# In a head pair's attention preparation: the queries' rotation first, then key norms and value blocks in turn

## The chip, the core and the metric

The program runs on one core of a Trainium2 chip. The metric is the device time of one execution in microseconds (us). The kernel before takes 3843.91 us (median of three runs, 3839.26 to 3847.75).

## What is computed

The reference runs four residual blocks (a gated unit, an RWKV-7 scan, a latent attention, a second gated unit) and then a second network (a gated linear scan with a convolution, and a mixture of 16 experts) on 512 tokens of width 1024. The change touches the latent attention alone: 16 heads, 512 queries, 768 keys (256 of the context, 512 of the sequence), and both queries and keys are normalised over 192 features, 64 of which are rotated.

```python
def mla_project(h, w_in, q_norm, kv_norm, w_uq, w_ukv, qk_gain_q, qk_gain_k, need_q):
    ...
    q = (rms_norm(c_q, q_norm) @ w_uq).reshape(bsz, length, MLA_HEADS, MLA_QK_DIM)
    q = rms_norm(q, qk_gain_q)
    ...
    kv = (rms_norm(c_kv, kv_norm) @ w_ukv).reshape(bsz, length, MLA_HEADS, MLA_NOPE + MLA_VDIM)
    k_nope, v = jnp.split(kv, [MLA_NOPE], axis=-1)
    k = jnp.concatenate([k_nope, jnp.broadcast_to(k_rope[:, :, None, :], ...)], axis=-1)
    k = rms_norm(k, qk_gain_k)
...
    s = jnp.concatenate([jnp.einsum('bqhd,bkhd->bhqk', qp, k_ctx), jnp.einsum('bqhd,bkhd->bhqk', qr, k_rot)], axis=-1)
    p = jax.nn.softmax(s.astype(jnp.float32) * MLA_SCALE, axis=-1).astype(v.dtype)
    return jnp.einsum('bhqk,bkhd->bqhd', p[..., :n_ctx], v_ctx) + jnp.einsum('bhqk,bkhd->bqhd', p[..., n_ctx:], v)
```

## The kernel before

Float32 products are made of three passes over a high and a low part (`mm3`, L169): an operand is split by a ScalarE copy into the high part and a subtraction on VectorE (`split`, L165) or GpSimd (`gsplit`, L2164) into the low part.

The attention's stage (L2144 to L2594) walks over 64 units, a unit being one head and 128 queries. `scores(u)` (L2439) makes 128 x 768 scores in a PSUM tile `ps2`, of which there is one buffer, so the next unit's scores can't be written before this unit's exponential has read it. VectorE takes the row maximum (L2455) and scales it (L2456), ScalarE makes the exponential (L2458) and scales it by the reciprocal of its sum (L2461 on VectorE, L2462 on ScalarE). `trans(u)` (L2465) turns the probabilities with six TensorE transposes (L2475) in two parts, 512 and 256 wide, and splits them into `a_pt` (L166 on ScalarE, L167 on VectorE). `av` (L2487) multiplies two units by the values. Other PSUM tiles (`ps`) come from a ring of six banks.

`prep(i)` (L2209) prepares a pair of heads while the units of the pair before are worked on. It is a generator; each of its steps puts matmuls first and hands the engines that follow their work one step later (`Work.step`, `Work.after`). `fill` (L2554) takes steps of it between scores, products and transposes, paced by the cost that each `yield` states. No scheduler reorders anything: every engine runs its queue in the order in which the generators wrote it. The steps of a pair, in order:

- keys' and queries' projections (`k_part`, `q_part`), then `slow.append(k_rstd())` and the second head's queries;
- `k_rstd` (L2302): a chain of small VectorE instructions (L2304, L258 to L270; tiles `rk_x`, `rk_t`, `rk_y` of 128 x 12) that makes the keys' inverse norms, and two ScalarE copies (L2310) that spread them into tiles called `rx`. `trickle(1)` puts a piece of it behind every step, and `trickle(99)` (L2315) the rest at once;
- `rot()` (L2345): the queries' rotated part, one product with a permutation (L2348) and the sums `q_sum(2)`; then VectorE L2353 and L2367, ScalarE L2360, GpSimd L2352 and L2362;
- `keys(2)`, `keys(0)`, `keys(1)` (L2318): the keys' norms turned and broadcast by transposes (L2325, 512 and 256 wide), multiplied on VectorE (L2329 for the rotated part, L2332 for a head), split by ScalarE L2165 and GpSimd L2166 into `a_krr` or `a_kn`;
- `q_sum(1)`, sums of the queries' squares on TensorE (L2274);
- three value blocks (L2389): twelve matmuls each, split by ScalarE L2403 and VectorE L2405 into `a_v`. After the first, `slow.append(q_rstd())`: the chain of some 16 small VectorE instructions (L2377, L2379, L2382, L258 to L270, L2387; tiles `a_c`, `rq_x`, `rq_t`, `rq_y` of 128 x 8) that makes the queries' inverse norms `rqs`, one of which goes behind each step.

The first pair has no units to lie between. Where this text says pair 4, it is the fifth of eight, whose rotation stands at 2209.8 us.

Of the kernel before, what the change touches and what calls it, by code (L numbers as in the profile page):

```python
# [106 lines left out]
KD = 450  # L107
KTR = 0.5
RG = 0
ORD = "p201"  # L110
AHEAD = 0.6
AVP = 1
NTR = 1
# [5 lines left out]
class Net:  # L119
# [1834 lines left out]
    def mla(self):  # L1954
# [228 lines left out]
        slow = []  # L2183

        def trickle(n):

            while slow and n > 0:
                c = next(slow[0], None)
                if c is None:
                    slow.pop(0)  # L2190
                n -= 0 if n == 99 else c or 1
# [5 lines left out]
        def o_load(c):  # L2197
            t = t5()
            nc.sync.dma_start(t, d_o[c])
            s8 = mp.tile([P, 2, TX], F32R, name="cq", bufs=6) if c < 6 else mp.tile([P, 2, TT], F32R, name="ckv", bufs=2)[:, :, :TX]  # L2200
            S8.append((s8, t))
# [7 lines left out]
        def prep(i):  # L2209
# [59 lines left out]
            def q_sum(j):  # L2269
                sq = sqs.pop(j)  # L2270
                for t_ in range(4):
                    tk = slice(t_ * P, (t_ + 1) * P)
                    if j < 2:
                        nc.tensor.matmul(pq[:, 4 * t_ + j:4 * t_ + j + 1], sq[:, tk], self.ones[:, :1], start=True, stop=True)  # L2274
                    else:
                        nc.tensor.matmul(pq[:, 4 * t_ + 2:4 * t_ + 4], sq[:, tk], bones[:, 0:P:64], start=True, stop=True)
# [35 lines left out]

            slow.append(k_rstd())
            yield from q_part(1, q_head(1))
            trickle(99)  # L2315
            rk = R["rk"]

            def keys(j):  # L2318
                for s0, s1 in ((0, 4), (4, 6)):
                    rx_ = rx.pop(0) if j == 2 else None  # L2320
                    o, w = s0 * P, (s1 - s0) * P
# [46 lines left out]
                parts(1, r)  # L2368
                yield 0

            for c in ORD:
                yield from rot() if c == "p" else keys(int(c))
            q_sum(1)

            def q_rstd():
                c4 = tl("c4", (P, 4, 4), 2)
                V.tensor_copy(c4.rearrange("p t c -> p (t c)"), pq[:, :16])  # L2377
# [8 lines left out]
                R["rqs"] = tl("rqs", (P, 8), 2)  # L2386
                V.tensor_scalar(R["rqs"], rq, 192 ** -0.5, None, op0=OP.mult)  # L2387

            for t2 in range(3):  # L2389
                ps = self.psum()  # L2390
                for tt in range(2):
                    t_ = 2 * t2 + tt
# [11 lines left out]
                for j, vv in enumerate(R["v"]):  # L2404
                    V.tensor_tensor(vv[:, 1, ts, :], p4[:, :, j * P:(j + 1) * P], vv[:, 0, ts, :], op=OP.subtract)  # L2405
                if i == H // 2 - 1:
                    for c in ((0, 1, 2, 3), (), (4, 5, 6, 7))[t2]:
                        o_load(c)
                    for c in ((), (0, 1), (2, 3))[t2]:
                        o_split(c)  # L2410
                if t2 == 0:
                    slow.append(q_rstd())
                if t2 == 2:
                    for _ in range(2 if i < H // 2 - 1 else 1):
                        wnext()
                yield 0

        def out_first():

# [1519 lines left out]
```

## Time and profile before

| what | us |
|---|---|
| median of three runs | 3843.91 |
| the profiled execution | 3851.94 |
| its span | 3850.0 |
| preparation of the first pair's tail, then the 64 units | about 1958 to 2510 |
| TensorE busy in the whole span | 3335.9 (87%) |

The profiled execution lies 8.03 us over the median and 1.94 us over its own span. In the rows, a time is in us from the span's start; `PE` is TensorE, `DVE` VectorE, `ACT` ScalarE, `POOL` GpSimd. In the order of work, a bracket such as [1.57 <-ACT a_t L2310] says how long the engine stood idle before the instruction, and which instruction ended the idle time. An `x2` merges two instructions of a kind, and the duration is then that of both.

### The profile page before, as it was taken

The page shows a single profiled execution, that of the slowest core. Times are in us where ns is not written, and L with a number is a line of the kernel's source. Part 1 is how long each engine was busy: PE and PEld are TensorE (multiplying, and loading weights), DVE is VectorE, ACT ScalarE, POOL GpSimd, SP SyncE. Part 2 cuts the span into 40 slices and gives each one's busy share as a digit, 9 for nine tenths or more (in the row PEclk, how much of TensorE's full clock was granted, in tenths as well). Part 3 has the DMA queues.
Part 4 walks back from the last instruction along what each step waited for, and adds up shares of the span by engine and source line. Part 5 has one row for each costly group of instructions (what it writes and reads, how often), then busy time and mean ns, then how long its engine had stood idle before and what let it go on. Part 6 is the DMA issues. An engine that isn't in the chain of part 4 may idle for free. (4 is left out here: it accounts for less than half of the span.)

```text
span 3850.0 us, 63102 instructions
## 1 busy us (share of the span) xinstructions
PE 3335.9 (87%) x24502; PEld 2816.5 (73%) x24502; DVE 2505.5 (65%) x4375; ACT 1710.7 (44%) x2887; POOL 1317.8 (34%) x1559
## 2 busy tenths in 40 slices
PE   4999998888688889989989999899998886778883
PEld 3788887777577778767878878777886665667773
DVE  8777767453676666745445555556666789777777
ACT  4322213433455545645346666533232543346663
POOL 5131002220356666720033332301101556235555
PEclk8999998999797788989999999999999997779997
DMA  5444452246874343463422122345642210289883
GB/s 194 151 145 140 140 198 95 85 166 179 247 196 133 117 141 112 136 204 123 124 72 73 56 66 64 106 140 200 219 159 73 72 55 17 81 288 315 314 308 119
DMA packets 350861, 560.23 MB, mean 146 GB/s; under 512 B 170592, under 2 KB 226016, under 8 KB 350560
## 3 DMA queue, kind: packets, MB, share of 16 engines
q1 hardware_dynamic: 346960, 543.06, 43.5%
q0 software_dynamic: 3600, 13.11, 0.9%
q8 instruction: 194, 3.18, 0.3%
q14 instruction: 107, 0.88, 0.1%
HBM read 457.23 MB, written 88.36 MB: 142 GB/s over the span
## 5 line engine op out<-in xcount | busy, mean ns | idle before, releaser
L162 DVE TENSOR_TENSOR wlo<-wraw,whi 128x1024 fp32r<-128x1024 f32 x220 | 286.2, 1301 | 165.1 <-ACT whi L161 163.6
L171 PE MATMUL ps<-hl,whi 128*128 128x512 f32 (+1 forms) x992 | 363.7, 367 | 1.6 <-ACT hl L1946 1.6
L161 ACT CAST whi<-wraw 128x1024 fp32r<-128x1024 f32 x221 | 231.3, 1047 | 294.4 <-PE ps L172 183.1
L172 PE MATMUL ps<-hl,whi 128*128 128x512 f32 (+1 forms) x992 | 360.2, 363 | 2.0 <-DVE hl L1951 2.0
L173 PE MATMUL ps<-hl,wlo 128*128 128x512 f32 (+1 forms) x992 | 359.6, 363 | 2.6 <-DVE wlo L162 2.6
L3583 ACT CAST e_wsp<-mraw 128x1024 fp32r<-128x1024 f32 x204 | 212.3, 1050 | 105.1 <-issue 52.5
L3584 DVE TENSOR_TENSOR e_wsp<-mraw,e_wsp 128x1024 fp32r<-128x1024 f32 x136 | 187.3, 1399 | 73.0 <-ACT e_wsp L3583 71.6
L3584 POOL TENSOR_TENSOR e_wsp<-mraw,e_wsp 128x1024 fp32r<-128x1024 f32 x68 | 180.0, 2656 | 129.6 <-ACT e_wsp L3583 59.2
L173 PEld LDWEIGHTS ps<-hl,wlo 128*128 128x128 f32 x992 | 187.3, 189 | 34.9 <-DVE wlo L162 3.4
L172 PEld LDWEIGHTS ps<-hl,whi 128*128 128x128 f32 x992 | 187.3, 189 | 34.1 <-DVE hl L1951 4.1
L171 PEld LDWEIGHTS ps<-hl,whi 128*128 128x128 f32 x992 | 187.3, 189 | 31.8 <-ACT hl L1946 1.9
L1522 POOL TENSOR_TENSOR s_tmp<-s_N,s_P 128x15 f32<-128x15 f32 (+4 forms) x360 | 126.6, 352 | 167.8 <-DVE s_N L1506 141.5
L207 DVE SCALAR_TENSOR_TENSOR araw<-araw,conds 128x1024 f32<-128x1024 f32 x128 | 157.8, 1238 | 24.7 <-DMA araw<-ada 24.0
L171 PE MATMUL ps<-whi,hl 128*128 128x512 f32 x320 | 131.8, 412 | 27.5 <-ACT hl L404 25.8
L617 POOL TENSOR_SCALAR v<-v,vr_y 128x256 f32<-128x256 f32 x70 | 93.9, 1359 | 155.8 <-DVE vr_y L270 155.8
L171 PE MATMUL ps<-s,whi 128*128 128x512 f32 (+1 forms) x384 | 138.6, 361 | 0.0
L172 PE MATMUL ps<-s,whi 128*128 128x512 f32 (+1 forms) x384 | 136.7, 356 | 0.0
L173 PE MATMUL ps<-s,wlo 128*128 128x512 f32 (+1 forms) x384 | 136.6, 356 | 0.2 <-DVE wlo L162 0.2
L167 DVE TENSOR_TENSOR a_pt<-ps,a_pt 128x512 fp32r<-128x512 f32 (+1 forms) x128 | 69.2, 554 | 102.3 <-ACT a_pt L166 102.3
L172 PE MATMUL ps<-wlo,hl 128*128 128x512 f32 x320 | 131.8, 412 | 4.5 <-DVE wlo L162 4.3
L173 PE MATMUL ps<-whi,hl 128*128 128x512 f32 x320 | 131.6, 411 | 1.4 <-DVE hl L411 1.3
L1523 POOL TENSOR_TENSOR s_P<-s_P,s_tmp 128x15 f32<-128x15 f32 (+4 forms) x360 | 121.4, 337 | 28.2
(932 smaller groups left out, 10195.2 us busy)
## 6 DMA issues: line engine op xcount, KB each, us to landing
mraw<-moe_w SPq DMA_DIRECT2D x204, 512.0 KB, 5.3
araw<-ada SPq DMA_DIRECT2D x144, 512.0 KB, 3.9
wraw<-sgu_v SPq DMA_DIRECT2D x40, 512.0 KB, 3.4
wraw<-rw_in SPq DMA_DIRECT2D x40, 512.0 KB, 4.8
d_n<-ff SPq DMA_DIRECT2D x48, 384.0 KB, 5.2
s_fn<-d_n SPq DMA_DIRECT2D x24, 768.0 KB, 6.5
wraw<-sgu_out SPq DMA_DIRECT2D x34, 512.0 KB, 4.2
wraw<-sgu_u SPq DMA_DIRECT2D x32, 512.0 KB, 4.6
```

The costliest lines, as they stand in the source:

```text
L161: self.nc.scalar.copy(hi[:, :cols], t[:, :cols])
L162: (eng or self.nc.vector).tensor_tensor(lo[:, :cols], t[:, :cols], hi[:, :cols], op=OP.subtract)
L167: (eng or self.nc.vector).tensor_tensor(lo, src, hi, op=OP.subtract)
L171: mm(out, lh, rh, start=start, stop=False)
L172: mm(out, lh, rl, start=False, stop=False)
L173: mm(out, ll, rh, start=False, stop=stop)
L207: self.nc.vector.scalar_tensor_tensor(junk, w, 0.5, c, op0=OP.mult, op1=OP.mult, accum_out=out)
L617: e.tensor_scalar(vt[g][:, t, :], vt[g][:, t, :], r[:, t:t + 1], None, op0=OP.mult)
L1522: TTG(o, N[:, None, ts, s].to_broadcast([P, nj, nt]), Pm[:, js, s:s + 1].to_broadcast([P, nj, nt]), op=OP.mult)
L1523: TTG(Pm[:, js, ts], Pm[:, js, ts], o, op=OP.subtract)
L3583: S.copy(hl[:, 0, :], raw)
L3584: (G if j % 3 == 2 else V).tensor_tensor(hl[:, 1, :], raw, hl[:, 0, :], op=OP.subtract)
```

## The change

In every pair: `rot()` comes directly behind the second head's queries, then `q_sum(1)`, then the rest of `k_rstd` (`trickle(99)`), then `q_rstd` is handed out, and then `keys(2)`, the first value block, `keys(0)`, the second value block, `keys(1)`, the third. Before, `trickle(99)` stood ahead of `rot()`, the three `keys` followed one another, and the value blocks stood behind all of them. In the last pair the loads of finished heads (`o_load`) are spread over the three value blocks as 2, 2 and 4 instead of 4, 0 and 4. No instruction's kind, size or engine is changed.

```diff
             slow.append(k_rstd())
             yield from q_part(1, q_head(1))
-            trickle(99)
-            rk = R["rk"]
 
             def keys(j):
+                rk = R["rk"]
...
-            for c in ORD:
-                yield from rot() if c == "p" else keys(int(c))
-            q_sum(1)
-
             def q_rstd():
...
-            for t2 in range(3):
+            def values(t2):
                 ps = self.psum()
...
                 if i == H // 2 - 1:
-                    for c in ((0, 1, 2, 3), (), (4, 5, 6, 7))[t2]:
-                        o_load(c)
                     for c in ((), (0, 1), (2, 3))[t2]:
                         o_split(c)
-                if t2 == 0:
-                    slow.append(q_rstd())
+                    for c in ((0, 1), (2, 3), (4, 5, 6, 7))[t2]:
+                        o_load(c)
...
+            yield from rot()
+            q_sum(1)
+            trickle(99)
+            slow.append(q_rstd())
+            for j, t2 in ((2, 0), (0, 1), (1, 2)):
+                yield from keys(j)
+                yield from values(t2)
```

(`ORD` was "p201": the rotation, then keys 2, 0, 1.) Line numbers in the changed kernel are one lower up to L2315; behind that they differ by more: L2309 is the copy into `rx`, L2459 the exponential, L2463 its scaling, L2397 and L2399 the split of a value block, L2327 and L2330 the keys' multiplications.

ScalarE in pair 4, from the copies into `rx` on. Before:

```order
L2310 COPY a_t_22289<-rk_y 128x512
L2310 COPY a_t_22291<-rk_y 128x256
L2458 ACTIVATE a_p,a_sm<-ps_22272,a_mx,a_rqs 128x768
L2462 ACTIVATE a_p<-a_p,a_sm 128x768
L2360 CAST a_qrr<-a_t_22160 64x512 x2
```

Now:

```order
L2459 ACTIVATE a_p,a_sm<-ps_22272,a_mx,a_rqs 128x768
L2309 COPY a_t_22303<-rk_y 128x512
L2309 COPY a_t_22305<-rk_y 128x256
L2463 ACTIVATE a_p<-a_p,a_sm 128x768
L2358 CAST a_qrr<-a_t_22160 64x512 x2
```

The two copies moved from ahead of a unit's exponential to behind it.

ScalarE in pair 4 between the next two exponentials. Before:

```order
L2458 ACTIVATE a_p,a_sm<-ps_22351,a_mx,a_rqs 128x768
L2462 ACTIVATE a_p<-a_p,a_sm 128x768
L2165 CAST a_krr<-a_t_22377 64x256 x2
L2165 CAST a_kn<-a_knf 128x512
L2165 CAST a_kn<-a_knf 128x256
L166 CAST a_pt<-ps 128x4x128
L2165 CAST a_kn<-a_knf 128x512
L166 CAST a_pt<-ps 128x2x128
L2458 ACTIVATE a_p,a_sm<-ps_22441,a_mx,a_rqs 128x768
```

Now:

```order
L2459 ACTIVATE a_p,a_sm<-ps_22358,a_mx,a_rqs 128x768
L2463 ACTIVATE a_p<-a_p,a_sm 128x768
L2164 CAST a_krr<-a_t_22390 64x256 x2
L2397 CAST a_v<-ps 128x256 x2
L2164 CAST a_kn<-a_knf 128x512
L165 CAST a_pt<-ps 128x4x128
L2164 CAST a_kn<-a_knf 128x256
L165 CAST a_pt<-ps 128x2x128
L2459 ACTIVATE a_p,a_sm<-ps_22471,a_mx,a_rqs 128x768
```

A value block's two casts stand ahead of the keys' casts, and the keys' 256-wide cast stands between the two casts of the probabilities.

VectorE in the same place, from the reciprocal to the next maximum. Before:

```order
L2461 RECIPROCAL a_sm<-a_sm 128x1
L2329 TENSOR_TENSOR a_t_22377<-krot,ps 128x256
L2332 TENSOR_TENSOR a_knf<-a_knf,ps 128x512
L2332 TENSOR_TENSOR a_knf<-a_knf,ps 128x256
L2495 SCALAR_TENSOR_TENSOR a_o<-ps,a_z 128x256
L167 TENSOR_TENSOR a_pt<-ps,a_pt 128x4x128
L2332 TENSOR_TENSOR a_knf<-a_knf,ps 128x512
L167 TENSOR_TENSOR a_pt<-ps,a_pt 128x2x128
L2455 TENSOR_REDUCE a_mx<-ps_22441 128x1
```

Now (twelve of its rows; two more small ones and `a_pt` 128x2x128 follow before the maximum):

```order
L2327 TENSOR_TENSOR a_t_22390<-krot,ps 128x256
L259 TENSOR_SCALAR rq_t<-rq_x 128x8
L2399 TENSOR_TENSOR a_v<-ps,a_v 128x256 x2
L261 TENSOR_SCALAR rq_y<-rq_t 128x8
L262 TENSOR_SCALAR rq_x<-rq_x 128x8
L2330 TENSOR_TENSOR a_knf<-a_knf,ps 128x512
L265 TENSOR_TENSOR rq_t<-rq_y 128x8
L2496 SCALAR_TENSOR_TENSOR a_o<-ps,a_z 128x256
L267 TENSOR_TENSOR rq_t<-rq_t,rq_x 128x8
L166 TENSOR_TENSOR a_pt<-ps,a_pt 128x4x128
L269 SCALAR_TENSOR_TENSOR rq_y<-rq_t,rq_y 128x8
L2330 TENSOR_TENSOR a_knf<-a_knf,ps 128x256
```

The value block's subtractions came ahead of the keys' multiplication, the keys' second multiplication behind the first half of `a_pt`, and the queries' chain between them.

## Rows read from the trace of the kernel before

**Rows 1.** Busy time by engine, 2000 to 2450: busy (x count), TensorE's clock, DMA.

```profile
core 0: us, PE busy (x) PEld busy (x) DVE busy (x) ACT busy (x) POOL busy (x), PEclk, DMA share, GB/s
2000.00:2450.00 450.00, 408.76 (x2562) 357.78 (x2561) 244.74 (x616) 280.69 (x551) 161.37 (x139) 0.96 0.24 68
```

**Rows 2.** TensorE's waits, 1958 to 2460: waiting line, releaser, total us, times, longest.

```profile
PE ps L2325 <- ACT a_t L2310: 19.5, 8, 5.7
PE ps L2325 <- DVE a_t L2329: 6.8, 6, 1.5
PE ps L171 <- DVE a_pt L167: 6.7, 3, 2.3
PE ps L171 <- ACT a_p L2458: 6.5, 11, 2.3
PE ps L2325 <- DVE a_pt L167: 4.4, 4, 1.5
PE ps L2220 <- ACT a_t L2232: 1.7, 1, 1.7
```

**Rows 3.** TensorE in order of time, pair 4: start, us, instruction, idle before.

```profile
2213.71 1.11 PE L2325 MATMUL ps<-ident,a_t 128*128 128x128 f32 x4 [1.57 <-ACT a_t L2310]
...
2233.65 0.50 PE L171 MATMUL ps<-a_kn,a_qn 128*128 128x512 f32 x1 [0.43 <-ACT a_p L2458]
...
2241.68 0.48 PE L171 MATMUL ps<-a_kn,a_qn 128*128 128x512 f32 x1
```

**Rows 4.** ScalarE in order of time, pair 4, four exponentials and what lies between.

```profile
2213.04 0.92 ACT L2310 COPY a_t<-rk_y 128x512 f32<-128x512 f32 x2 [4.11 <-DVE rk_y L270]
2214.22 0.99 ACT L2458 ACTIVATE a_p<-ps,a_mx,a_rqs 128x768 f32<-128x768 f32 x1 [0.26 <-DVE a_mx L2456]
...
2215.54 0.94 ACT L2462 ACTIVATE a_p<-a_p,a_sm 128x768 f32<-128x768 f32 x1 [0.23 <-DVE a_sm L2461]
...
2224.20 0.99 ACT L2458 ACTIVATE a_p<-ps,a_mx,a_rqs 128x768 f32<-128x768 f32 x1 [1.67 <-DVE a_mx L2456]
...
2226.35 0.82 ACT L2165 CAST a_krr<-a_t 64x256 fp32r<-64x256 f32 x2
...
2228.03 0.58 ACT L166 CAST a_pt<-ps 128x512 fp32r<-128x512 f32 x1
2229.96 0.62 ACT L2165 CAST a_kn<-a_knf 128x512 fp32r<-128x512 f32 x1 [1.35 <-DVE a_knf L2332]
2230.48 0.37 ACT L166 CAST a_pt<-ps 128x256 fp32r<-128x256 f32 x1
2232.52 0.99 ACT L2458 ACTIVATE a_p<-ps,a_mx,a_rqs 128x768 f32<-128x768 f32 x1 [1.67 <-DVE a_mx L2456]
...
2234.97 0.64 ACT L2403 CAST a_v<-ps 128x256 fp32r<-128x256 f32 x2
...
2239.50 0.99 ACT L2458 ACTIVATE a_p<-ps,a_mx,a_rqs 128x768 f32<-128x768 f32 x1 [2.58 <-DVE rq_t L260]
```

**Rows 5.** VectorE in order of time, pair 4.

```profile
2228.64 0.69 DVE L167 TENSOR_TENSOR a_pt<-ps,a_pt 128x512 fp32r<-128x512 f32 x1 [1.58 <-ACT a_pt L166]
2229.25 0.68 DVE L2332 TENSOR_TENSOR a_knf<-a_knf,ps 128x512 f32<-128x512 f32 x1
2230.88 0.42 DVE L167 TENSOR_TENSOR a_pt<-ps,a_pt 128x256 fp32r<-128x256 f32 x1 [0.96 <-ACT a_pt L166]
2231.22 0.95 DVE L2455 TENSOR_REDUCE a_mx<-ps 128x1 f32<-128x768 f32 x1
...
2235.64 0.76 DVE L2405 TENSOR_TENSOR a_v<-ps,a_v 128x256 fp32r<-128x256 f32 x2 [1.53 <-ACT a_v L2403]
```

**Rows 6.** First pair, in order of time: TensorE, then VectorE, then GpSimd.

```profile
1965.75 1.54 PE L2325 MATMUL ps<-ident,a_t 128*128 128x128 f32 x6 [5.65 <-ACT a_t L2310]
...
1978.64 0.94 DVE L2382 COPY a_c<-a_c 128x8 f32<-128x8 f32 x1
...
1982.26 0.17 DVE L266 TENSOR_TENSOR rq_t<-rq_y 128x8 f32<-128x8 f32 x1
...
1976.30 3.96 POOL L2166 TENSOR_TENSOR a_kn<-a_knf,a_kn 128x512 fp32r<-128x512 f32 x4
```

More of the change, by code (lines that the diff above doesn't have):

```diff
@@ L109 @@
 RG = 0
-ORD = "p201"
 AHEAD = 0.6
```

## The prediction

> **What bounds the kernel now.** I read the busy times of the attention's stage first, then the list of what TensorE waited for, then the order of work of each engine around one rotation. From 2000 to 2450 us TensorE is busy 408.76 of 450 us at a mean clock of 0.96 [rows 1]; the stage ends when TensorE's queue ends, so only its idle time (41 us) and its slow stretches can change. The waits are few and all lie around the rotation and the keys: 19.5 us for the copies of the key norms (L2310, once per pair, 5.65 us of it in the first pair [rows 6]), 6.8 and 4.4 us in the keys' transposes, which wait for PSUM banks that VectorE reads late, 6.7 us of products that wait for the split probabilities, and 6.5 us of scores that wait for an exponential [rows 2].
>
> The last of these is the row to look at. The scores' PSUM tile has one buffer, so each unit's scores wait for the exponential of the unit before. Call the four exponentials of pair 4 E0 (2214.22, beside the rotation), E1 (2224.20), E2 (2232.52) and E3 (2239.50) [rows 4]. The scores behind E2 start at 2233.65 after 0.43 us of waiting for it [rows 3]: in the middle of the preparation the chain of ScalarE and VectorE from one exponential to the next is already as long as TensorE's own work. E1 to E2 is 8.32 us. The next scores, at 2241.68, carry no wait [rows 3]: E3 came 2.18 us before them, and that stretch of 8.03 us is TensorE's.
>
> **The change part by part.** No instruction is added or removed, so what counts is the place of each in its queue. Pairs 1 to 7 lie among units, the first does not.
>
> (a) The copies into the key-norm tiles now stand behind E0 on ScalarE. They take 0.92 us and were hidden ahead of E0; there ScalarE now waits 0.23 us less for the reciprocal [rows 4], so everything behind E0 comes 0.92 - 0.23 = 0.69 us later. On VectorE two small instructions of the queries' chain now stand ahead of E1's maximum, at 0.17 us each [rows 6]: 0.34 us. E0 itself comes some 0.2 us earlier, since the last small instruction of the keys' chain moves behind its maximum (0.17 us by the same row). Sum: 0.8 us later at E1. TensorE's wait for these copies becomes longer too (they came 1.18 us before E0, now 1 us behind it), but that costs nothing of its own: the queue is then bound by E1 and E2 anyway.
>
> (b) E1 to E2 is the main term. What must happen there in a row, because each engine takes its queue in order, is this. From E1 to the cast of the rotated keys: 2224.20 to 2226.35, 2.15. That cast: 0.82. The value block's casts until VectorE can subtract: 2234.97 to 2235.64, 0.67. The subtractions: 0.76. The keys' multiplication until its cast: 2229.25 to 2229.96, 0.71. That cast until the cast of the probabilities: 2229.96 to 2230.48, 0.52. From there to VectorE: 2228.03 to 2228.64, 0.61. To the keys' second multiplication: 2228.64 to 2229.25, 0.61. Its cast, and the next cast of probabilities, 256 wide: no more than the 0.71 and 0.52 of the 512-wide ones; I take 0.5 and 0.3. To VectorE: 2230.48 to 2230.88, 0.40. To the maximum: 0.34. To E2: 2231.22 to 2232.52, 1.30 [rows 4, 5]. Together 9.7, and four small instructions of the queries' chain between them, some 0.5 at 0.1 to 0.17 each: 10.2 us, against 8.32. Before, the value block was not in this stretch, and one keys' multiplication of the two was ready ahead of time. Cost 1.9 us, and since the scores behind E2 wait for E2 already, all of it comes through.
>
> (c) E2 to E3 has the same row without the rotated keys' cast: 9.7 - 0.8 + 0.4 = 9.3 us. Before it was 6.98 us and hidden under TensorE's 8.03. The scores behind E3 therefore come about 1.2 us later once more. TensorE has the same work behind it in both kernels, and runs without a wait there, so it doesn't win the time back.
>
> (d) What the value blocks fill. Moved between the keys, one block covers the products' wait and the keys' waits for banks. This saves TensorE's idle time at those rows, but the scores that follow wait for E2 and E3, so it is worth nothing while (b) and (c) hold. If they didn't, it would be the first rival.
>
> (e) The queries' chain meets GpSimd. L2382, a copy of 128 x 8, took 0.94 us while GpSimd worked through four subtractions (3.96 us), and an instruction of the same size took 0.17 us at 1982.26, when those were over [rows 6]. Before, most of this chain ran behind the keys' subtractions; now it runs among them and on the way to E1, E2 and E3. An instruction that meets one pays up to 0.94 - 0.17 = 0.8 us. Four or five stand on the way; most find GpSimd idle, since its subtraction follows a cast that VectorE waits beside. Bounds 0 and 4 us per pair; I take 0.5, near the lower one, since at most one of them falls inside a subtraction in the row of (b).
> The Trainium skill, page "SBUF — State Buffer", section "Who interferes with whom", says that an instruction of VectorE with two SBUF inputs, or a copy or scalar operation in a two-port mode, and one of GpSimd that reads SBUF exclude each other for the whole instruction. The 0.94 us row agrees with it, and by that rule every small instruction of the chain is open to such a wait, which speaks against moving the chain here.
>
> Per pair: 0.8 + 1.9 + 1.2 + 0.5 = 4.4 us, between 2.5 (a part of (a) and (c) absorbed by small overlaps) and 6.5 (two or three stalls of (e), and scores at a slower clock behind the longer waits). Seven pairs: 31 us, from 17 to 46.
>
> (f) The first pair. TensorE waited 5.65 us there for the key norms [rows 6]. The rest of the keys' chain now stands behind the rotation's addition, which waits for GpSimd, and then meets four of GpSimd's subtractions of the rotated queries: between 1.3 us (addition and multiplication alone) and 5 us later. Against it, TensorE fills some 1.6 us of the wait with the queries' sums, and the queries' norms are ready earlier, which saves up to the 1.7 us for which L2220 waited behind the first exponential [rows 2], and a stretch at slow clock behind it, about as much again. From -4 to +4; I take +0.5.
>
> (g) The last pair's loads go to the same queue in twos instead of fours, earlier than they are used. Taken as zero: no row of the waits shows TensorE held by them [rows 2].
>
> Sum: 31 + 0.5, about 31 us. On the profiled execution's 3851.94 that is 3883; that execution lies 8.03 us over the median, so against the median of 3843.91 it is 3875. Own range: 17 - 4 to 46 + 4, 3857 to 3894.
>
> **The rivals.**
>
> *The blocks fill the holes, and the exponentials keep up.* If the row of (b) is shorter than I added up, because casts and subtractions overlap more than one engine's order lets me see, TensorE stays the bound, and the waits for banks and probabilities go: 6.8 + 6.7 + 4.4, with the 1.7 of the first pair some 20 us. That gives 3824. It decides itself at E1 to E2: at or under 8.3 us it holds. For it: TensorE is the busiest engine by far (408.76 against 280.69 for ScalarE [rows 1]). Against it: every step of (b) hangs on the one before or stands behind it in its queue.
>
> *It evens out.* (b) holds but (c) doesn't, the units behind regain part, and the filled holes and the first pair's gain return the rest: 7 x 1.9 less about 10 us, 3845 to 3848.
>
> *The stalls of (e) are the rule.* Each small instruction on the way meets a subtraction: four times 0.8 per pair more than taken, less the 0.5: 2.7 x 7 = 19 us on top, 3894, and with slower clock behind the longer holes up to 3905.
> The Trainium skill's page "SBUF — State Buffer", same section, would make this the expected case wherever the two engines' work overlaps.
>
> **How the numbers follow.** Forecast 0.67, first rival 0.13, second 0.12, third 0.08. One can tell about 0.2%, 7.7 us, from no change for this kernel. Faster is the first rival, 0.13. The second is within 0.2% but for a sixth of it, which is slower: same 0.10. Slower is the rest: 0.77. The range runs from no change, with half of what can be told below it, to the third rival's lower end: 3840 to 3894, leaving out the first rival and most of the third, some 0.2. The time is the forecast's, 3875.
>
> **What would show it.** In pair 4 of the changed kernel: E1 to E2 near 10 us (8.3 now), E2 to E3 near 9.3 (7.0 now), and scores behind E2 and E3 that wait 2 to 4 and about 1 us for an exponential; TensorE's waits for L2310 up, for L2329 and the probabilities down, those for the exponential from 6.5 to over 25 us. The copies into the norm tiles start right behind E0. The prediction is wrong if E1 to E2 stays near 8.3 us, or if the stage from the first rotation to the last product gets shorter.

## The result, and the profile after

The changed kernel takes 3880.16 us, the median of five runs (3868.86 to 3887.28), against 3843.91 us (3839.26 to 3847.75): the ratio is 1.0095, with a 95% interval of 1.008 to 1.0109. That is 36 us more, between 31 and 42. The profiled execution of the changed kernel has a span of 3880.5 us.

Runs of one kernel differ by ten microseconds and more in the parts of the program that nothing here touches: in the profiled executions of this study the first rotation starts anywhere from 1938 to 1964 us. So beside each time stands a second measure that excludes those parts, the stretch from the first exponential of the attention stage to its last one (64 of them). It is 517.48 us before and 548.01 us after: 30.5 us of the 36 are there. Another 2.2 us lie in the first pair, between its rotation and the first exponential (27.15 us before, 29.37 us after, from starts of L2348 and L2458 before, L2346 and L2459 after). Lines have moved by one to eight numbers: L2458 is now L2459, L2310 is L2309, L2329 is L2327, L2403 is L2397, L2405 is L2399.

First the busy time of a stretch as long as in [rows 1]. The columns are those of that group.

```profile
1999.00:2449.00 450.00, 396.34 (x2419) 350.78 (x2419) 230.00 (x579) 262.45 (x513) 145.69 (x127) 0.92 0.21 59
```

TensorE is busy 396.34 us where it was busy 408.76, its mean clock is 0.92 in place of 0.96, and it finishes 2419 matmul records in place of 2562. TensorE's waits from 1958 to 2500 us, against [rows 2]:

```profile
PE ps L2323 <- ACT a_t L2309: 31.3, 8, 10.0
PE ps L170 <- ACT a_p L2459: 23.0, 8, 3.1
PE ps L2476 <- DVE a_t L2327: 8.8, 6, 2.0
PE ps L170 <- DVE a_v L2399: 4.3, 7, 0.7
PE ps L170 <- ACT cq L165: 3.2, 1, 3.2
```

The waits for the key norms' copies grew from 19.5 to 31.3 us, those of scores for an exponential from 6.5 to 23.0. The waits of [rows 2] for banks and for split probabilities (6.8, 6.7 and 4.4) are no longer in the list, but others took their place: the transposes of the probabilities wait 8.8 us for a bank that the rotary keys' multiplication (L2327) still reads, and matmuls wait 4.3 us for one that a value block's subtraction (L2399) still reads. Pair 4 on TensorE, against [rows 3]:

```profile
2229.88 1.11 PE L2323 MATMUL ps<-ident,a_t 128*128 128x128 f32 x4 [2.69 <-ACT a_t L2309]
...
2250.72 0.80 PE L170 MATMUL ps<-a_kn,a_qn 128*128 128x512 f32 x1 [3.12 <-ACT a_p L2459]
...
2260.19 0.48 PE L170 MATMUL ps<-a_kn,a_qn 128*128 128x512 f32 x1
```

The scores behind E2, which had 0.43 us to wait, wait 3.12 us. ScalarE in the same pair, against [rows 4]:

```profile
2228.24 0.99 ACT L2459 ACTIVATE a_p<-ps,a_mx,a_rqs 128x768 f32<-128x768 f32 x1 [5.07 <-DVE rk_y L269]
...
2229.23 0.91 ACT L2309 COPY a_t<-rk_y 128x512 f32<-128x512 f32 x2
2230.04 0.94 ACT L2463 ACTIVATE a_p<-a_p,a_sm 128x768 f32<-128x768 f32 x1
...
2239.51 0.99 ACT L2459 ACTIVATE a_p<-ps,a_mx,a_rqs 128x768 f32<-128x768 f32 x1 [2.40 <-DVE a_mx L2457]
...
2249.59 0.99 ACT L2459 ACTIVATE a_p<-ps,a_mx,a_rqs 128x768 f32<-128x768 f32 x1 [1.76 <-DVE rq_y L269]
...
2258.58 0.99 ACT L2459 ACTIVATE a_p<-ps,a_mx,a_rqs 128x768 f32<-128x768 f32 x1 [1.67 <-DVE a_mx L2457]
```

E0, E1, E2 and E3 are 11.27, 10.08 and 8.99 us apart, where they were 9.98, 8.32 and 6.98. The copies stand right behind E0. E4 to E7 are the exponentials of the four units behind E3, up to the next pair's E0.

All kernels of this study side by side, in starts of the exponentials of pair 4 (the last interval of the turn before it, then its first three, then the sum from E1 to E7). The same intervals repeat in pairs 5 and 6 within a few hundredths in most kernels; pairs 2 and 3 had a first interval of only 8.84 us in the kernel before. The column from E1 to E7 is pair 4's alone and differs between the pairs, as said below. The e, g and h kernels and k1 are edits of the changed kernel and keep its spread of the last pair's loads, also where they are described as the kernel before with one change.

| kernel | first to last | E7 to E0 | E0 to E1 | E1 to E2 | E2 to E3 | E1 to E7 | ratio of times, 95% |
|---|---|---|---|---|---|---|---|
| before | 517.5 | 10.93 | 9.98 | 8.32 | 6.98 | 45.3 | 1 |
| after | 548.0 | 10.75 | 11.27 | 10.08 | 8.99 | 48.5 | 1.0095 (1.0080 to 1.0109) |
| e1_norms_first | 545.6 | 10.94 | 10.76 | 10.06 | 8.99 | 48.5 | 1.0086 (1.0058 to 1.0113) |
| e2_chain_late | 542.0 | 10.73 | 10.44 | 9.71 | 9.12 | 48.6 | 1.0070 (1.0043 to 1.0097) |
| e3_keys_in_a_row | 540.7 | 10.72 | 11.22 | 9.49 | 6.90 | 48.7 | 1.0054 (1.0033 to 1.0074) |
| e4_turns_alone | 541.1 | 10.94 | 9.97 | 9.59 | 9.12 | 48.5 | 1.0094 (1.0066 to 1.0121) |
| g1_one_turn | 532.8 | 10.93 | 9.98 | 9.59 | 6.48 | 46.9 | 1.0035 (1.0018 to 1.0051) |
| g2_late_split | 540.7 | 10.73 | 11.23 | 9.33 | 7.86 | 48.4 | 1.0074 (1.0052 to 1.0096) |
| h1_copies_late | 519.6 | 10.74 | 10.45 | 8.31 | 6.91 | 45.5 | 1.0015 (0.9995 to 1.0034) |
| f2_chain_quick | 516.4 | 11.71 | 9.97 | 8.32 | 6.98 | 45.3 | 1.0015 (0.9997 to 1.0032) |
| f3_plain_keys_first | 520.6 | 10.93 | 9.21 | 9.08 | 6.98 | 46.1 | 1.0007 (0.9989 to 1.0025) |
| k1_after_filled | 547.7 | 10.73 | 11.25 | 10.07 | 9.00 | 48.5 | 1.0098 (1.0072 to 1.0123) |
| k2_before_filled | 516.5 | 10.93 | 9.98 | 8.32 | 6.98 | 45.3 | 0.9989 (0.9972 to 1.0005) |
| m1_chain_before_weights | 497.3 | 8.09 | 9.96 | 8.32 | 6.98 | 45.3 | 0.9912 (0.9892 to 0.9932) |

Each ratio is against runs of the kernel before in the same job, whose medians lay between 3837.75 and 3853.20 us. An expectation that names a time is therefore judged by its distance from the kernel before.

### The profile page after: what moved, and what is told of

It reads as the page before. It is cut to its first block, busy times and chain, and to the rows that moved or that the text cites. A ratio compares the mean times of both kernels' runs of the same rounds, so it can differ in the third digit from the quotient of the medians.

```text
span 3880.5 us, 63131 instructions
## 1 busy us (share of the span) xinstructions
PE 3345.7 (86%) x24502; PEld 2825.3 (73%) x24502; DVE 2510.3 (65%) x4375; ACT 1711.8 (44%) x2887; POOL 1320.8 (34%) x1559
```

## Experiments: which part of the change costs

The theory: the turns of keys and values cost most, the late copies and the early chain of the query norms a little each. The rival: one of the moved chains is the cause, and the turns are harmless.

**e1_norms_first.** The changed kernel with the key norms ahead of the rotation again:

```diff
-            yield from rot()
-            q_sum(1)
             trickle(99)
+            yield from rot()
+            q_sum(1)
```

> The changed kernel with one thing put back: the rest of the key-norm chain and its two ScalarE copies are issued ahead of the rotation again; the turns of keys and values, and the early query norms, stay. Theory (each moved piece pays in the interval of its own, and the turns pay most): in pairs 2 to 7 the first interval between exponentials falls from 11.26 us to 10.2 to 10.5, the second and third stay at 10.1 and 9.0, the first wait of TensorE for the copies in the first pair falls from 9.96 to about 5.7; seven times 0.8 to 1.0 and 2 to 4 in the first pair, so 3869 to 3873 us against 3880. Rival (the late copies are the cause, and the longer intervals behind them only follow from them): all three intervals go back and the time is at most 3855.

Measured: 1.0086; the first interval falls by 0.5 us, the second and third stay, the first pair's wait for the copies goes from 10.0 to 4.8 us, and the stretch gets 2.4 us shorter. The rival's return of all three intervals did not come. The gain in the interval is the theory's mechanism at half its size; the time, 33 us over the kernel before where 25 to 29 were expected, can't be told from the changed kernel's.

**e2_chain_late.** The changed kernel with the chain of the query norms queued behind the second value block only:

```diff
-            slow.append(q_rstd())
             for j, t2 in ((2, 0), (0, 1), (1, 2)):
                 yield from keys(j)
                 yield from values(t2)
+                if t2 == 1:
+                    slow.append(q_rstd())
```

> The changed kernel with the chain of the query norms queued only behind the second block of values, so that it no longer lies beside the rotation's GpSimd work. Theory (the collision of the small VectorE operations with GpSimd is worth about 0.5 us a pair): seven times 0.5, so 3874 to 3879 us, the first interval at about 10.8 us, the second and third unchanged. Rival (the chain's collision is most of the loss): at most 3862, with the first interval back under 10.2 us.

Measured: 1.0070, the stretch 6.0 us shorter, the first interval 0.8 us and the second 0.4 us shorter. That is nearly twice the theory's 3.5 us and far from the rival's 18. The row that pays in the changed kernel, on VectorE in pair 4, is the first of these two; the second is the maximum that it holds up:

```profile
2237.49 0.82 DVE L2376 COPY a_c<-a_c 128x8 f32<-128x8 f32 x1
2238.22 0.95 DVE L2456 TENSOR_REDUCE a_mx<-ps 128x1 f32<-128x768 f32 x1
```

**e3_keys_in_a_row.** The changed kernel without the turns:

```diff
-            for j, t2 in ((2, 0), (0, 1), (1, 2)):
+            for j in (2, 0, 1):
                 yield from keys(j)
+            for t2 in range(3):
                 yield from values(t2)
```

> The changed kernel with the turns undone: rotation, then the key norms' copies and the query norms as in the changed kernel, but the three key blocks in a row and then the three value blocks. Theory (the turns of keys and values are what costs): the second and third intervals go back to about 8.3 and 7.0 us and the first stays at 11 to 11.3; what is left is seven times 1.3 and 1 to 4 in the first pair, so 3852 to 3858 us. Rival (the turns are harmless, the place of the norms and the rotation is the cause): 3872 to 3880, the second and third intervals still over 9 us.

Measured: 1.0054, 21 us over the kernel before, where the theory wanted 8 to 14; the stretch is still 23 us longer than before. The third interval went back as expected, the second stayed at 9.49 where 8.3 was expected. The theory fell in this point: without the turns most of the loss is still there. VectorE on the way to E1 (first row) and to E2 (the next two) shows why, then TensorE behind E2, and last the stretch of TensorE from these scores to the next (columns as in [rows 1]):

```profile
2231.22 0.79 DVE L2376 COPY a_c<-a_c 128x8 f32<-128x8 f32 x1
2238.26 0.59 DVE L269 SCALAR_TENSOR_TENSOR rq_y<-rq_t,rq_y 128x8 f32<-128x8 f32 x1
2240.74 0.74 DVE L267 TENSOR_TENSOR rq_t<-rq_t,rq_x 128x8 f32<-128x8 f32 x1
2243.83 0.80 PE L170 MATMUL ps<-a_kn,a_qn 128*128 128x512 f32 x1 [3.11 <-ACT a_p L2460]
...
2243.83:2254.64 10.81, 10.81 (x58) 10.05 (x59) 5.54 (x18) 7.89 (x18) 2.51 (x3) 0.72 0.03 10
```

With the keys in a row GpSimd's subtractions follow each other closely, and the small steps of the chain (0.16 us when nothing is beside them) meet three of them on the way to E1 and E2. E2 is late, and the scores behind it wait 3.11 us as in the changed kernel. Behind that wait TensorE, without a gap, takes 10.81 us at a mean granted clock of 0.72 for what takes it 8.03 us at 1.00 in the kernel before. Over pairs 1 to 6 this one stretch is 61.3 us against 48.3: 13 of the 23 us.

**h1_copies_late.** What of e3 are the copies, what the chain? The kernel before with the late copies alone, here as an edit of the changed kernel:

```diff
             yield from rot()
+            trickle(99)
+            for j in (2, 0, 1):
+                yield from keys(j)
             q_sum(1)
-            trickle(99)
+            yield from values(0)
             slow.append(q_rstd())
-            for j, t2 in ((2, 0), (0, 1), (1, 2)):
-                yield from keys(j)
-                yield from values(t2)
+            yield from values(1)
+            yield from values(2)
```

> The kernel before with one thing of the change alone: the rest of the key-norm chain and its two ScalarE copies are issued behind the rotation; the keys stand in a row, the values behind them, and the query norms where they were. Theory (the late copies cost what putting them back into the changed kernel gave, 0.5 us in the first interval and some us in the first pair, and the rest of what the run without turns still lost belongs to the query norms' chain beside the keys' GpSimd work): the stretch from first to last exponential 519 to 522 us against 517.5, the first interval of pairs 4 to 7 at 10.4 to 10.6 us, the second and third at 8.3 and 7.0; the time 2 to 6 us over the kernel before. Rival (the copies are what the run without turns lost): 537 us or more, the time 15 us or more over.

Measured: 1.0015, the stretch 2.2 us longer, the first interval 10.45. The theory holds in each number. So the copies are worth 2 us of stretch, and the remaining 21 us of e3 come with the early sums and chain of the query norms.

**e4_turns_alone.** The kernel before with the turns alone, again as an edit of the changed kernel:

```diff
+            trickle(99)
             yield from rot()
-            q_sum(1)
-            trickle(99)
-            slow.append(q_rstd())
             for j, t2 in ((2, 0), (0, 1), (1, 2)):
                 yield from keys(j)
+                if t2 == 1:
+                    q_sum(1)
                 yield from values(t2)
+                if t2 == 1:
+                    slow.append(q_rstd())
```

> The turns of keys and values alone on the kernel before: key norms, rotation and the query norms (two steps behind the first value block's work) stand as they did, only each key block is followed by a value block. Theory (the turns cost, whatever comes ahead of them): the first interval stays at about 10 us, the second and third are at about 10 and 9, the next at 7.7 instead of 9.3, and one interval later is 1 longer; seven times 3 to 3.5, so 3864 to 3869 us. Rival (the turns are harmless): 3843 to 3850.

Measured: 1.0094, with intervals of 9.97, 9.59 and 9.12 and a stretch of 541.1 us, 23.6 us longer. The interval behind E3 is 9.10 and not the expected 7.74, and no later one grew. The stretch is as expected; the time is 36 us (25 to 46) over the kernel before, where 20 to 25 were expected, and what lies outside the stretch is open. The turns alone are enough for most of the loss, too. In this kernel the scores behind E2 wait for nothing; TensorE loses its time earlier, where its transposes wait for a bank that the first value block's subtraction still reads (TensorE, then VectorE; 16.6 us in all, in seven waits):

```profile
2237.92 0.69 PE L2478 MATMUL ps<-ident,a_p 128*128 128x128 f32 x2 [2.40 <-DVE a_v L2399]
...
2237.11 0.76 DVE L2399 TENSOR_TENSOR a_v<-ps,a_v 128x256 fp32r<-128x256 f32 x2 [2.07 <-ACT a_v L2397]
```

**g1_one_turn.** One value block moved and not two: after the rotary keys comes the first value block, then `keys(0)`, `q_sum(1)`, `keys(1)`, `values(1)`, the chain, `values(2)`.

> The kernel before with one turn alone: the first value block stands between the rotary keys and the first head's keys, the other two behind all keys as before; the query norms' chain is queued behind the second value block. Theory (each displaced value block costs its own interval): half of what two displaced blocks cost in the run with the turns alone, whose stretch from the first to the last exponential was 541 against 517 us: 527 to 532 us, the second interval at 9.6 us as there, the third back to 7 to 8.3, and the time 10 to 15 us over the kernel before. Rival (one block is covered, only the second overfills): under 521 us, time the same as before within 4 us.

Measured: 1.0035, the stretch 15.3 us longer, just over the theory's upper edge; the second interval 9.59 as with both blocks, the third 6.48. One displaced block costs about two thirds of what two cost (15.3 of 23.6 us): as much from E1 to E7 in pairs 1 to 3, half in pairs 4 to 6.

**g2_late_split.** The changed kernel, TensorE's order kept, with the value block's ScalarE and VectorE work moved back:

```diff
                 if t2 == 0:
                     R["v"] = [tl("v", (P, 2, 6, P), 3, F32R) for _ in range(2)]
+                def part():
...
+                held.append(part)
+                if t2 == 2:
+                    part_now()
...
                             nc.sync.dma_start(dst[RW[rows.start == 0]].bitcast(F32), dst[rows].bitcast(F32))
+                    if s0:
+                        part_now()
                     yield 0
```

Here `part` holds the two casts and the two subtractions, and `part_now` calls what is held.

> The changed kernel with TensorE's order kept, but the two casts and two subtractions of each value block are queued on ScalarE and VectorE only behind the work of the key block that follows it. Theory (what the turns cost is the value block's casts and subtractions, which stand between the key work and the row maximum of the unit, and not TensorE's order): the second interval falls from 10.1 to 9 or less, the third from 9.0 to 8 or less, seven times 1.5 to 2, so 12 to 16 us under the changed kernel. Rival (the value block's accumulator, held until its split is done, is what TensorE waits for): the intervals stay or grow, since the buffer is held longer; time as the changed kernel or up to 15 us over it.

Measured: 1.0074. The second interval falls by 0.75 us, to 9.33 where 9 or less was wanted, and the third by 1.1 us, to 7.86 as expected. The place of the casts and subtractions is worth 1.9 of the 3.8 us by which E1 to E3 had grown; they still stand between E1 and E2, so the rest is not told apart. In time half of what the theory wanted came: the stretch is 7.3 us shorter than the changed kernel's, where 12 to 16 were expected. In pair 4 the two intervals from E4 to E6 grew from 6.79 and 8.42 to 7.59 and 9.47 and took the gain back; in pairs 1, 2, 3 and 5 E1 to E7 stayed 1.0 to 2.4 us shorter than in the changed kernel.

In pair 4 the column from E1 to E7 has 48.4 to 48.7 us in every kernel in which the chain or both blocks are moved, and 45.3 to 45.5 where neither is (46.1 with the keys in another order, 46.9 with one block moved). It is no constant of these kernels: over pairs 1 to 6 it runs from 47.6 to 49.3 in the changed kernel, from 46.7 to 48.7 in e3, from 47.6 to 49.3 in e4, from 46.9 to 48.5 in g1 and from 45.2 to 48.5 in g2, against 44.4 to 45.4 before. What repeats is that TensorE has hardly a gap from the scores behind E2 to those behind E7, at most 0.6 us in pair 4 of any kernel, so lateness at E2 can't be made up. TensorE in before and after, from the scores behind E2 to those behind E3:

```profile
2233.65:2241.68 8.03, 8.03 (x59) 7.53 (x59) 4.43 (x16) 5.04 (x12) 0.74 (x1) 1.00 0.17 59
...
2250.72:2260.19 9.47, 9.47 (x59) 8.71 (x59) 4.60 (x14) 4.63 (x10) 2.03 (x2) 0.84 0.02 6
```

The same 59 matmul records, without a gap in either, take 9.47 us in place of 8.03, at a mean granted clock of 0.84 between its two levels: before them stood the wait of 3.12 us. The two stretches divided where the scores end, before and then after:

```profile
2233.65:2235.51 1.86, 1.86 (x11) 1.64 (x12) 0.46 (x2) 1.68 (x5) 0.37 (x1) 1.00 0.65 231
2235.51:2241.68 6.17, 6.17 (x51) 5.89 (x49) 3.97 (x14) 3.36 (x9) 0.37 (x1) 1.00 0.02 7
...
2250.72:2253.97 3.25, 3.25 (x11) 2.77 (x12) 1.65 (x6) 1.58 (x4) 0.00 (x0) 0.53 0.03 13
2253.97:2260.19 6.22, 6.22 (x51) 5.95 (x49) 2.95 (x8) 3.05 (x7) 2.03 (x2) 1.00 0.01 3
```

The scores take 3.25 us in place of 1.86, at a mean clock of 0.53, near the lower of the two levels (1.2 GHz); the rest, at 1.00 (2.4 GHz), takes 6.22 and 6.17. So of the 3.2 us by which E1 to E7 grew in pair 4, 1.76 stand at E1 to E2 and 1.44 here, nearly all of them at the lower clock. In pairs 1 to 6 the stretch takes 9.5 to 10.9 us against 8.0 to 8.1 before, 11.5 us together of the 30.5. That the wait lowers the clock was not tested: no run filled this wait.

The chain and the turns together cost hardly more than each alone (30.5 us of stretch against 21 and 23.6). The traces show that the single kernels lose their time in different ways, e3 at this lower clock and e4 in waits for a bank, but not why the sums lie so close.

## Experiments: TensorE's waits and its clock

**k1_after_filled** and **k2_before_filled** put idle matmuls where TensorE waits. The edit of k1; k2 has the same function and the numbers that its expectation names:

```diff
+            def warm(n):
+                for _ in range(n):
+                    nc.tensor.matmul(pq[:, 256:512], ckv[0][:, 0, :P], ckv[0][:, 0, :256], start=True, stop=True)
...
                     o, w = s0 * P, (s1 - s0) * P
+                    warm({(2, 0): 20}.get((j, s0), 0) if i else {(2, 0): 60}.get((j, s0), 0))
                     pb = self.psum()
```

> The changed kernel with 20 idle matmuls (128x256, their result is read by nobody) in front of the rotary keys' transposes in each pair, 60 in the first, where TensorE waits 2.69 and 9.96 us for ScalarE's copies; the computation is the same. Theory (part of the loss is the clock that TensorE is granted after such a wait): the wait is filled, the granted clock behind it stays at full speed, TensorE's work of the next intervals takes less, 3 to 8 us under the changed kernel. Rival (these intervals are set by the chain of exponential, transposes, split and maximum, in which TensorE has slack): no change, or up to 5 us over it.

> The kernel before with idle matmuls of the same kind where TensorE waits: 12 in front of the rotary keys' transposes, 10 in front of the second half of the first head's keys, 10 in front of the second head's keys, 40 in the first pair; the computation is the same. Theory (the waits cost twice, once by their length and once by the lower clock after them): the granted clock of the stretch goes from 0.96 to 0.98 or more and the time 4 to 10 us under the kernel before. Rival (TensorE has slack there): the same within 4 us, or up to 8 us over it where the filling delays a transpose.

The stretch from first to last exponential (columns as in [rows 1]) of after, k1, before and k2:

```profile
1984.32:2532.33 548.01, 485.24 (x2916) 426.60 (x2915) 278.19 (x681) 316.34 (x610) 173.50 (x146) 0.93 0.23 67
...
1980.99:2528.64 547.65, 493.60 (x3056) 432.72 (x3055) 274.26 (x681) 316.28 (x610) 173.44 (x146) 0.96 0.23 67
...
1985.44:2502.92 517.48, 471.73 (x2911) 411.40 (x2910) 275.93 (x681) 314.77 (x611) 173.28 (x146) 0.96 0.25 70
...
1968.57:2485.06 516.49, 488.74 (x3151) 431.55 (x3150) 275.96 (x681) 314.79 (x611) 173.52 (x146) 0.99 0.24 71
```

In k1 the wait for the copies shrank from 31.3 to 6.3 us and the clock rose from 0.93 to 0.96, in k2 from 0.96 to 0.99, and the intervals of the exponentials did not move: 11.25, 10.07 and 9.00, and 9.98, 8.32 and 6.98. The time of k2 alone would not exclude 4 to 10 us less (0.9972 to 1.0005 is 11 us less to 2 more), but its stretch is only 1.0 us shorter. Both rivals hold. The waits for the copies, and the clock behind them, are slack of TensorE; they were no cost before, and are none after. The wait for E2 was not filled, so the clock behind that one stays untested.

**f2_chain_quick**: `KTR = 0.25` in place of 0.5 in the kernel before, so that four and not two steps of the key norms' chain are queued at a time.

> The kernel before with the chain of the key norms let in twice as fast (four small steps at a time in place of two), so that more of it is done before GpSimd's long subtraction and rotation product stall it. Theory (the chain's late end is what TensorE's wait for the two copies comes from): the wait of 1.57 us a pair shrinks, the first interval of pairs 4 to 7 goes from 9.98 to 8.8 us as in pairs 2 and 3, so 5 to 10 us under the kernel before. Rival (the steps are stalled all the same, or stall the row maximum): no change within 4 us.

Measured: 1.0015, no change that can be told. TensorE's waits from 1958 to 2520 us:

```profile
PE ps L171 <- ACT a_p L2458: 17.7, 13, 2.3
...
PE ps L2325 <- ACT a_t L2310: 1.1, 3, 0.4
```

The wait for the copies is gone (19.5 to 1.1 us) and came back as a wait for the exponential (6.5 to 17.7). The first interval stayed at 9.97: the theory fell.

**f3_plain_keys_first**: `ORD = "p021"` in the kernel before, the first head's keys ahead of the rotary ones.

> The kernel before with the first head's keys ahead of the rotary keys: the transposes that need no copies from ScalarE go first, so that the copies are done beside them. Theory (TensorE's wait for the copies is 19.5 us in all and part of it is the copies' own 0.9 us): the first interval 0.5 to 1 us shorter, 3 to 7 us under the kernel before. Rival (the rotary keys, with their GpSimd subtractions and their DMA, then end too late, and their two stretches collide with the third interval): 5 to 15 us over it.

Measured: 1.0007. The first interval is 0.77 us shorter, the second 0.76 us longer. It evens out in these intervals: the theory's 3 to 7 us less did not come. The stretch is 3.1 us longer, and the time's interval (4 us less to 10 more) does not exclude the lower end of the rival's 5 to 15.

## Experiment: a version that beats both

f2 had one interval that told more. Ahead of pairs 1 to 5 the interval E7 to E0 grew from 10.93 to 11.7 us, but ahead of pair 6 it was 10.77 (11.22 in the kernel before), and ahead of the last pair 8.88, where the kernel before has 11.94. What stands in that interval in the kernel before, here ahead of pair 4, is the key norms' chain beside GpSimd (two rows of VectorE, two of GpSimd):

```profile
2207.98 2.11 DVE L270 SCALAR_TENSOR_TENSOR rk_y<-rk_t,rk_y 128x12 f32<-128x12 f32 x1
2210.12 1.19 DVE L266 TENSOR_TENSOR rk_t<-rk_y 128x12 f32<-128x12 f32 x1
...
2207.66 2.40 POOL L2166 TENSOR_TENSOR wlo<-wraw,whi 128x1024 fp32r<-128x1024 f32 x1 [6.02 <-PE ps L173]
2210.01 1.27 POOL L2352 TENSOR_TENSOR a_t<-a_t,rope 128x512 f32<-128x512 f32 x1
```

Two steps of 12 columns, 0.17 us each when alone, take 2.11 and 1.19 us: each ends when GpSimd's instruction does. **m1_chain_before_weights** sets `KTR = 0.16` in the kernel before: seven steps at a time, and the chain is over before the weights come.

> The kernel before with the chain of the key norms let in seven small steps at a time, so that all of it stands on VectorE before GpSimd's long subtraction of the next weights (2.4 us) begins; with four at a time one step still stood beside it and took 2.24 us, and the interval ahead of the pair grew from 10.94 to 11.7 us, but to 8.89 us in the one pair that has no such weights. Theory (the collision of one small VectorE step with that subtraction costs the interval ahead of each pair about 2 us): the interval from the last exponential of a pair's second head to the first of the next (10.94 us in the kernel before) falls to 8.5 to 9.3 us, the others stay, seven times 1.7 to 2.4, so 10 to 17 us under the kernel before. Rival (something else of the chain of exponential, split and maximum then ends as late, as when TensorE's waits were taken away): the same within 4 us.

One reason given there was wrong: the last pair has such weights too (in f2 GpSimd's subtraction starts at 2389.80 there). The interval was short because the chain, let in more often there, was over at 2386.8, three microseconds ahead of it. What the theory says of the collision is untouched by that.

Measured: 3817.32 us against 3853.20, a ratio of 0.9912 (0.9892 to 0.9932), 34 us less. E7 to E0 is 8.09 us, below the 8.5 to 9.3 that were expected, and the other intervals of the pair are as before: the theory's mechanism, at more than its size (10 to 17 us). The last step of the chain on VectorE in the turn ahead of pair 4, and GpSimd's subtraction:

```profile
2189.18 0.17 DVE L270 SCALAR_TENSOR_TENSOR rk_y<-rk_t,rk_y 128x12 f32<-128x12 f32 x1
...
2192.36 2.38 POOL L2166 TENSOR_TENSOR wlo<-wraw,whi 128x1024 fp32r<-128x1024 f32 x1 [7.12 <-ACT whi L2165]
```

The two stalls cost 2.11 + 1.19 - 2 x 0.17 = 2.96 us, and the interval fell by 2.84. The stretch from first to last exponential is 20.2 us shorter, and from the first rotation to the first exponential it is 2.1 us (25.03 in place of 27.15); the rest of the 34 us lies outside, where single executions differ by as much. The interval of the time, 26 to 42 us less, does not reach down to these 22, so what the rest is stays open. It was not measured beside the changed kernel; the two ratios put it 70 us ahead of that.

## Why the prediction came out right

The forecast was 3875 us, slower by 31; it became 3880, slower by 36, inside the forecast's own range. From one E0 to the next, pair 4's turn grew by 4.28 us (66.21 to 70.49), where the sum said 4.4. That it fits so closely is partly luck: the turns of pairs 1 to 6 grew by 3.8 to 6.3 us, 5.0 on average, the last pair only by 2.3, and one term of the sum came true by another mechanism than the one named. Step by step:

- **What bounds the kernel.** Here the reasoning was half right. "Only TensorE's idle time and its slow stretches can change" fails in k1, k2 and f2: idle time and slow stretches were removed there and the exponentials stayed where they were. In both kernels the chain of exponential, transposes, split and maximum on ScalarE and VectorE sets the time from E7 to E2, and TensorE has slack there; from the scores behind E2 to E7 TensorE is dense.
- **(a)** 0.8 at E1. The copies measured 0.5 (e1, h1) where 0.69 was worked out, and E0 came 0.2 earlier as said. E1 came 1.1 us later in all (1.29 less 0.18); what goes beyond 0.8 is a stall of the chain, which the sum has in (e).
- **(b)** 10.2 us from E1 to E2, measured 10.08. The turns alone give 9.59, the chain of the query norms the rest. The added row of steps was the right way to get this: ScalarE and VectorE of the changed kernel show every step of it in the order of the sum, none more than 0.23 us from its term, the small steps included.
- **(c)** 9.3 us from E2 to E3, measured 8.99, and 1.2 us at the scores behind E3, measured 1.44 (8.03 to 9.47). The interval is right. For the scores the mechanism isn't the one named: they don't wait for E3, TensorE itself takes 9.47 us for the same work at the clock of 0.84. The lower clock was put into the upper bound only, and it cost 1.4 to 2.8 us a pair in pairs 1 to 6; that pair 4's 1.44 lies near 1.2 is luck.
- **(d)** Holes filled are worth nothing: shown by k1 and k2. The changed kernel itself shows it less well, since other waits for banks took the place of those that were filled.
- **(e)** 0.5 us of stalls, between 0 and 4. In the changed kernel one step stalls in a pair's E0 to E1 (0.82 us) and few others; taking the chain away gave 0.8 and 0.4 us there (e2), of which the plain time of the steps was in (a) and (b). The term is right for the order that was built. But e3 shows how close the third rival was: without the turns the same chain met three subtractions.
- **(f)** +0.5 in the first pair, between -4 and +4. Its first exponential came 2.2 us later, the interval behind it 1.6 shorter (7.94 to 6.36): together 0.6. These are one profile each, and from the rotation to the first exponential the kernels with the late copies have 27.3 to 31.1 us, those with the early ones 25.0 to 27.2; so the sum is not known to better than 2 us. The wait for the norms grew by 4.3 us, inside the 1.3 to 5 that were taken. GpSimd's four subtractions (1960.83 to 1966.48) and one of the three small steps that they hold up:

```profile
1962.56 1.23 DVE L269 SCALAR_TENSOR_TENSOR rk_y<-rk_t,rk_y 128x12 f32<-128x12 f32 x1
...
1960.83 5.65 POOL L2360 TENSOR_TENSOR a_t<-a_t,a_qrr 64x512 fp32r<-64x512 f32 x4
```

- **(g)** The last pair's loads: no wait of TensorE names them after, either. The wait for ScalarE's split of these heads, `cq`, grew from 1.7 to 3.2 us, but that split stood in ScalarE's queue and did not wait for a load.
- What the sum left out: pairs 2 and 3 had a first interval of 8.84 us and lost 2.4 us there, not 1.3; pair 4 was taken for all. And that the parts don't add: by its own terms the sum gives some 18 us for the turns alone (7 x (1.4 + 1.2)) and 9 for the chain alone (7 x (0.3 + 0.5 + 0.5)), where they cost 23.6 and 21.
- The signs. The waits for an exponential came to 23.0 us and not over 25, seven times 3.1 us behind E2, once 1.2 behind E1 of the first turn, and none behind E3. The waits for the rotary keys' multiplication were to fall and rose, from 6.8 us (L2329) to 8.8 (L2327), at other transposes.
- The rivals. The first fell at E1 to E2 (10.08, not 8.3), the second, which let the scores behind E3 come on time, at the 9.47 us. The third, stalls as the rule, fell for this order. The Trainium skill, page "SBUF — State Buffer", section "Who interferes with whom", says that the instruction that comes first gets the shared pair of ports for its whole length, and the other one is blocked. The rows of 2.11 and 1.19 us above, which end with GpSimd's instructions, agree. What such stalls cost in this kernel lay mostly in another place than the one where it was looked for: the changed place of the query norms' chain is worth 6 us of stretch (e2), that of the key norms', which were there before, 20 (m1).

## What to carry to other kernels

Read a loop through the starts of its one serial instruction (here the exponential) and compare the intervals; a wait of the busiest engine is a cost only if filling or removing it moves them, and three times here it didn't. Work moved into an interval where another engine's chain is the bound costs its whole row of casts and subtractions, however idle the big engine looks there. Look for tiny VectorE steps that last exactly as long as the GpSimd instruction beside them: letting a chain of them run earlier, with no step removed, was worth more than any order of the large blocks.

## What the hardware showed that was not expected

- A step on 128 x 12 elements took 2.11 us beside a GpSimd subtraction of 128 x 1024 and 0.17 us without it; the kernel before has one such step of 1.86 to 2.40 us ahead of each of pairs 1 to 7, on the path.
- Raising TensorE's mean granted clock from 0.93 to 0.96 and from 0.96 to 0.99 by idle matmuls moved no interval between exponentials by more than 0.03 us in pair 4. After the wait of 3.12 us, in a stretch that TensorE fills, the clock of 0.84 went with 1.44 us more for the same 59 matmul records. The two are no contradiction: it depends on which engine the interval belongs to.
